# Seven block products in all three down products, roots by ScalarE, and the first up weights split ahead of the sums

## The chip, the cores and the metric

The kernel runs on one NeuronCore of a Trainium2 chip. TensorE (PE) multiplies matrices into PSUM, VectorE (DVE) and ScalarE (ACT) work on SBUF and PSUM, GpSimd (POOL) on SBUF, and SyncE (SP) issues nearly all DMAs. Each engine takes its instructions in a fixed order and waits on semaphores. The metric is the time of one execution on the device in microseconds (us), lower being better.

## The reference, cut to what matters

Two transformer blocks on 1024 tokens of width 1024, all in fp32. The first has three mixers (a state space model, a Fourier mixer, a banded attention) and a feed-forward part with a convolution over the tokens; the second has a feed-forward part, a two-branch attention, a second feed-forward part and a gate. The change touches the three feed-forward parts and the root in the norms:

```python
def rms_norm(x, gain):
    xf = x.astype(jnp.float32)
    y = xf * lax.rsqrt(jnp.mean(xf * xf, axis=-1, keepdims=True) + RMS_EPS)
    return (y * gain.astype(jnp.float32)).astype(x.dtype)
...
def dwconv3(h, w, b):
    hp = jnp.pad(h, ((0, 0), (1, 1), (0, 0)))
    return hp[:, :-2] * w[0] + hp[:, 1:-1] * w[1] + hp[:, 2:] * w[2] + b
...
        up = dwconv3(h @ w_up[l], conv_w[l], conv_b[l])          # first block, D_FF = 2816
        gate, val = jnp.split(up, 2, axis=-1)
        y = (jax.nn.gelu(gate) * val) @ w_down[l]
        x = x + gt_f * rms_norm(y, g_post_ffn[l])
...
def swiglu(x, w_gu, w_down):                                      # second block, twice
    g, u = jnp.split(x @ w_gu, 2, axis=-1)
    return (jax.nn.silu(g) * u) @ w_down
```

## The kernel before, in words

Every fp32 operand of a matmul is split into a high part (ACT copies it to fp32r) and a low part (DVE subtracts), and a product is three matmuls: high by high, low by high, high by low (`split`, L58 and L59; `mm3`, L96 to L98). The stages run one after another: the first mixer up to about 516 us, the feed-forward part with the convolution (ffn0 here) to about 1234, ffn1 to about 1885, the attention and its projection to about 2420, ffn2 and the gate to the end.

`ffn` is called for all three. It begins with four up tiles (hidden blocks 0 and 1) by plain products in four quarters of the tokens (`quarters`); their weights fill all four places of the tags `wh` and `wl`. Then it makes sums of the activation's quarters (L264 to L268, split into `S` and the `hl` of the old tiles), and for each further hidden block j a loop step: `weights(j)` loads two blocks of the up weight, makes four sums of them on POOL and splits all into `wh`, `wl` (three places each) and a tile `b`, and seven block products of 12 matmuls each (L297) stand for the eight of two by two blocks. `finish_tile` applies SiLU, or in ffn0 the convolution (L314 to L316) and GELU, and writes the block to DRAM.

For the down product ffn1 and ffn2 already use seven products (a Strassen scheme of Winograd's form): pairs of hidden blocks 2 to 19 in a group of four and one of five, seven chains of matmuls in each (`chain`, L445), fed by `blocks`, which loads the parts of a block one chain ahead (L431): parts of `hidden`, of the sums `hsum`, of `w_down` and of the sums `wsum`. The sums are made in the up loop. Of blocks 0, 1, 20 and 21 the product is plain and ends each part. ffn0 has no such sums and does all blocks in plain products of two blocks at a time (`down`), and the last four in one.

A part ends with its tail: for each of 8 token tiles the last sums into `yacc` (L406), the mean square on ACT (L145), a root on DVE (`rstd`, L121 to L128: a starting value from the integer bits and three Newton steps on 128x1 tiles), scaling (L1865), adding (L1866), a second mean square and root, the norm (L153) and transposes on PE (L180) split into `hh` and `hl` of the next part. `rstd` is called twice per tile.

The order of each engine's instructions is fixed when the kernel is built, by a scheduler that follows the code's order and data. Buffers are pools by tag: `raw` 3, `wh` and `wl` 4, `hh` and `hl` 2, `b4` (named `b` in the trace) 12. A tile that asks for a place waits for the last use of the tile before it.

Of the kernel before, what the change touches and what calls it, by code (L numbers as in the profile page):

```python
# [5 lines left out]
F32 = mybir.dt.float32  # L6
# [13 lines left out]
def f(ap):  # L20
    return ap.bitcast(F32)


class Core:
    def __init__(self, tc, ctx, ident, wbufs=4):
        self.tc, self.nc, self.ctx = tc, tc.nc, ctx
        nc = tc.nc
        self.g = ctx.enter_context(tc.tile_pool(name="g", bufs=1))
        self.ps = ctx.enter_context(tc.tile_pool(name="ps", bufs=1, space=PSUM))
        self.dr = ctx.enter_context(tc.tile_pool(name="dr", bufs=1, space=DRAM))  # L30

        for name, n, bufs in (("ss", 1, 4), ("rs_a", 1, 4), ("rs_i", 1, 4), ("rs_t", 1, 4), ("st0", 48, 2), ("st1", 48, 2)):
            self.g.tile([P, n], I32 if name == "rs_i" else F32, name=name, tag=name, bufs=bufs)
        self.A = [self.g.tile([P, 2, 24], F32, name=f"A{i}") for i in range(2)]
        self.taps = self.g.tile([P, 4, 44], F32, name="taps")
        self.cc = self.g.tile([P, 8], F32, name="cc")
        self.g.tile([P, 8], F32, name="gap")
        self.ones = self.g.tile([P, P], F32, name="ones")
        self.ident = self.g.tile([P, P], F32, name="ident")
        nc.sync.dma_start(self.ident, ident)  # L40
        self.wbufs = wbufs
        self.tmps, self.nrows = 4, 3
        self.pend = []
        self.tail = None
        self.rows = []
        self.tmptag = "tmp"
        self.counted = 0
# [69 lines left out]
    def rstd(self, ss):  # L117

        v = self.nc.vector
        s = self.g.tile([P, 1], F32, name="rs_a", tag="rs_a", bufs=4)  # L120
        v.tensor_scalar(s, ss, EPS, None, op0=OP.add)  # L121
        i = self.g.tile([P, 1], I32, name="rs_i", tag="rs_i", bufs=4)
        v.tensor_scalar(i, s.bitcast(I32), -0.5, float(0x5F3759DF), op0=OP.mult, op1=OP.add)
        y = i.bitcast(F32)
        t = self.g.tile([P, 1], F32, name="rs_t", tag="rs_t", bufs=4)
        for c in (3.0, 12.0, 768.0):
            v.tensor_scalar(t, y, y, s, op0=OP.mult, op1=OP.mult)  # L127
            v.tensor_scalar(y, t, c, y, op0=OP.subtract, op1=OP.mult)  # L128
        return y
# [54 lines left out]
def ffn(k, hT, w_gu, w_down, nff, prep, finish, taps=None, then=None):  # L184
# [5 lines left out]


    nc, v, pool = k.nc, k.nc.vector, k.nc.gpsimd
    pairs = list(range(2, nff - 2, 2)) if taps is None else []
    with k.tc.tile_pool(name="ffn", bufs=1) as fp:
        k.places(fp, "b4", 12)
        hidden = k.dr.tile([nff, P, D], F32, name=f"hidden{k.count()}")
        if pairs:
            hsum = k.dr.tile([2 * len(pairs), P, D], F32, name=f"hsum{k.count()}")
            wsum = k.dr.tile([2 * len(pairs), P, D], F32, name=f"wsum{k.count()}")

        def b4(dt=F32):
            return fp.tile([P, D], dt, name="b4", tag="b4", bufs=12)
# [54 lines left out]
        up, dn = slice(0, 4), slice(4, 8)  # L257
        A11, A12, A22, S4 = (h0[:, up], l0[:, up]), (h0[:, dn], l0[:, dn]), (h1[:, dn], l1[:, dn]), (h1[:, up], l1[:, up])
        S1, S2, S3 = [(t[:, 0], t[:, 1]) for t in sums]
        for a in range(0, 4, 2):  # L260
            c = slice(a, a + 2)
            x21, x22, x11, x12 = xs = [b4().rearrange("p (a b) -> p a b", a=2) for _ in range(4)]
            for x, (hi, lo) in zip(xs, (S4, A22, A11, A12)):
                v.tensor_tensor(x, f(hi[:, c]), f(lo[:, c]), op=OP.add)  # L264
            v.tensor_tensor(x22, x21, x22, op=OP.add)
            v.tensor_tensor(x21, x11, x21, op=OP.subtract)
            v.tensor_tensor(x11, x22, x11, op=OP.subtract)
            v.tensor_tensor(x12, x12, x11, op=OP.subtract)  # L268
            for x, (hi, lo) in ((x22, S1), (x11, S2), (x21, S3), (x12, S4)):
                k.split(hi[:, c], lo[:, c], x)  # L270

        def weights(j):

            rg, rv = k.raw([P, 8, P]), k.raw([P, 8, P])
# [16 lines left out]
            return dict(B11=both(W1, up), B21=both(W1, dn), T1=both(W2, up), T2=both(W2, dn), T3=both(W3, up),  # L291
                        B22=both(W3, dn), T4=(t4[:, 0], t4[:, 1]))

        def prod(ps, w, x, start):
            for a in range(4):
                for n, (y, z) in enumerate(((0, 0), (0, 1), (1, 0))):
                    nc.tensor.matmul(ps, w[y][:, a], x[z][:, a], start=start and a == 0 and n == 0, stop=a == 3 and n == 2,  # L297
                                     skip_group_check=True)
# [3 lines left out]
        def finish_tile(j, A, w, s, V):  # L302

            prod(A, w["T4"], A22, False)
            if taps is None:
                nc.scalar.activation(s[:, hi], A, AF.Silu)
                v.tensor_tensor(s[:, hi], s[:, hi], V[:, hi], op=OP.mult)
            else:
                nc.scalar.activation(s[:, hi], A, AF.Copy)
                us = []  # L310
                for m, z in ((j, s), (j + nff, V)):
                    u = b4()
                    t = [taps[:, a, m:m + 1] for a in range(4)]
                    nc.scalar.activation(u, z, AF.Identity, bias=t[3], scale=t[1])  # L314
                    v.scalar_tensor_tensor(u[:, 1:], z[:, :D - 1], t[0], u[:, 1:], op0=OP.mult, op1=OP.add)
                    v.scalar_tensor_tensor(u[:, :D - 1], z[:, 1:], t[2], u[:, :D - 1], op0=OP.mult, op1=OP.add)  # L316
                    us.append(u)
                s = us[0]
                nc.scalar.activation(s, s, AF.Gelu_apprx_tanh)
                v.tensor_tensor(s, s, us[1], op=OP.mult)  # L320
            nc.sync.dma_start(hidden[j], s)
            if pairs:
                made[j] = s

        made = {}

# [19 lines left out]

        prev = None
        for j in range(2, nff):
            w = weights(j)
            A, B, C = k.mm(), None, None  # L350
            X = b4()
            prod(A, w["B11"], A11, True)
# [11 lines left out]
            nc.scalar.activation(X[:, hi], C, AF.Copy)  # L364
            prod(A, w["T2"], S2, False)
            nc.scalar.activation(X[:, lo], A, AF.Copy)
            if j - 2 in pairs:
                weight_sums(j - 2)
            if j - 3 in pairs:
                hidden_sums(j - 3)  # L370
# [13 lines left out]
        def load(j):  # L384
# [6 lines left out]
            w = k.wide()  # L391
            k.split(*w, r)
            return h + w

        def down(ready, first, last):
            for i in range(NT):
                t = slice(i * P, i * P + P)
                for n in range(2):
                    c = slice(n * 512, n * 512 + 512)
                    po = k.mm()  # L400
                    for a, (hh, hl, wh, wl) in enumerate(ready):
                        k.mm3(po, (hh[:, t], hl[:, t]), (wh[:, c], wl[:, c]), a == 0, a == len(ready) - 1)
                    if first:
                        nc.scalar.activation(yacc[i][:, c], po, AF.Copy)
                    else:
                        v.tensor_tensor(yacc[i][:, c], yacc[i][:, c], po, op=OP.add)  # L406
                if last:
                    finish(fp, i, yacc[i])
                    if i >= 4:
                        k.flush(2, 1)  # L410

        def sources(name, j):

# [23 lines left out]
        def group(first):  # L437

            def chain(banks, h, c, start, new):
                ops = next(ahead)  # L440
                for i, po in enumerate(banks):
                    t = slice(i * P, i * P + P)
                    for m, (x, y) in enumerate(ops):
# [20 lines left out]
            chain(U, 1, hi, False, False)  # L464
            chain(U, 1, lo, False, True)

        groups = [pairs[:len(pairs) // 2], pairs[len(pairs) // 2:]] if pairs else []
        if pairs:
            def one_ahead(g):
                was = next(g)  # L470
                for x in g:
                    yield was
                    was = x
                yield was

            ahead = one_ahead(blocks())
            for a in range(2):
                group(a == 0)
        plain = [j for j in range(nff) if j - j % 2 not in pairs]
        n = len(plain) - 4  # L480
        for j in range(0, n, 2):
            down([load(j) for j in plain[j:j + 2]], j == 0, False)
        rows = big([4, D], F32)
        k.rows = [rows[:, a] for a in range(3)]
        k.junk = rows[:, 3]
        prep(fp)
        down([load(j) for j in plain[n:]], False, True)
        k.close()
        if then is not None:
            then(fp)  # L490
        k.rows = []
# [372 lines left out]
def project(k, mT, w, order, prep, finish, nrows):  # L864
# [4 lines left out]
    with k.tc.tile_pool(name="proj", bufs=1) as pp:  # L869
# [3 lines left out]
        for kt in order:  # L873
            r = k.raw([P, D])
            nc.sync.dma_start(r, w[kt * P:(kt + 1) * P, :])
            wh = pp.tile([P, D], F32R, name=f"woh{kt}")
            wl = pp.tile([P, D], F32R, name=f"wol{kt}")
            k.split(wh, wl, r)
            ws[kt] = (wh, wl)
        for i in range(NT):  # L880
            t = slice((i % 4) * P, (i % 4) * P + P)
            hi, lo = mT[i // 4]
# [13 lines left out]
            k.flush(1)  # L896
            finish(pp, i, y)
        k.close()

# [424 lines left out]
def mixers1(k, x, ada, p, prep, finish):  # L1326
# [345 lines left out]
    with tc.tile_pool(name="zo", bufs=1) as zo:  # L1672
# [13 lines left out]
                    next(gate, None)  # L1686

        prev = None
        for i in range(NT):
            y = k.tmp(zo)  # L1690
            for n, po in enumerate(product(i, (7, 0, 1, 2) if i < len(yp) else (3, 4, 5, 6, 7, 0, 1, 2))):
# [7 lines left out]
            prev = y  # L1699
        close(NT - 1, prev)  # L1700
        k.close()
    part.__exit__(None, None, None)
    outer.__exit__(None, None, None)
    return tabs
# [262 lines left out]
```

## Time and profile before

| | |
|---|---|
| median of 3 runs | 3171.17 us (3169.51 to 3174.13) |
| profiled execution, its own time | 3171.55 us |
| its span, first to last instruction | 3169.8 us |
| PE busy | 3027.8 us, 96% |
| DVE, ACT, POOL busy | 2156.8, 1327.4, 570.2 us |
| mean granted clock of PE | 0.978 of 2.4 GHz |

The span is one execution; all times in rows count from its start. Busy times are averages over stages of quite different kind, so the stages are read apart, in the rows further down.

### The profile page before, as it was taken

What the parts mean: (1) busy time and instruction counts of PE and PEld (TensorE: products, weight loads), DVE (VectorE), ACT (ScalarE), POOL (GpSimd) and SP (SyncE); (2) the same over time, 40 slices, a digit from 0 to 9 for tenths busy, and PEclk for the clock granted to TensorE, in tenths of its full rate; (3) what the DMA queues carried; (4) which work ended last, traced back from release to release, by engine and by line L of the source; (5) the groups of instructions that cost most, each with busy time, mean ns of one, the idle gap of its engine ahead of it and who ended that gap; (6) DMA issues with size and microseconds to landing.
All of it is one profiled execution on the core that took longest, in us unless ns stands there. A gap on an engine that the chain in (4) does not pass through costs nothing.

```text
span 3169.8 us, 40772 instructions
## 1 busy us (share of the span) xinstructions
PE 3027.8 (96%) x15146; PEld 2472.9 (78%) x15146; DVE 2156.8 (68%) x3750; ACT 1327.4 (42%) x2029; POOL 570.2 (18%) x823
## 2 busy tenths in 40 slices
PE   5889989799999998999999989999999999999998
PEld 3667668688887887888888878777779888888887
DVE  7866669866666669655556676666678655556687
ACT  4334643445444113433335434555742433335333
POOL 3468700222220000222220000000000222220000
PEclk8899999899999999999999999999999999999999
DMA  7474455122224232344458432210451344458434
GB/s 210 165 206 154 145 171 160 60 80 83 84 88 145 87 127 100 120 166 160 159 191 298 143 121 87 67 45 32 163 205 67 127 159 160 166 199 302 157 132 160
DMA packets 323578, 447.83 MB, mean 141 GB/s; under 512 B 40167, under 2 KB 213479, under 8 KB 323378
## 3 DMA queue, kind: packets, MB, share of 16 engines
q1 hardware_dynamic: 314914, 430.68, 40.7%
q10 hardware_dynamic: 6576, 9.00, 0.8%
q0 software_dynamic: 1888, 5.53, 0.7%
q8 instruction: 119, 1.95, 0.2%
q14 instruction: 81, 0.66, 0.1%
HBM read 322.02 MB, written 129.41 MB: 142 GB/s over the span
## 4 chain that ended last, share of the span: by engine, by line
PE 76%; DVE 9%; POOL 5%; DMA 2%; ACT 2%; issue 2%; ACTq 0%; DVEq 0%; SPq 0%; POOLq 0%
PE mm L297 36%; PE mm L445 9%; PE mm L96 7%; PE mm L98 7%; PE mm L97 7%; PE tp L445 2%; PE mm L644 2%; PE mm L606 2%; PE tp L632 2%; POOL X L1204 1%; POOL st L1201 1%; POOL X L1203 1%; POOL st L1202 1%; DVE rs_t L127 1%; DVE tmp L1866 1%
## 5 line engine op out<-in xcount | busy, mean ns | idle before, releaser
L297 PE MATMUL mm<-S,wh 128*128 128x512 f32 x1440 | 444.4, 390 | 8.1 <-ACT wh L58 4.9
L278 POOL TENSOR_TENSOR b<-raw 128x512 f32<-128x512 f32 x60 | 77.7, 1294 | 1485.4 <-PE tp L180 788.2
L58 ACT ACTIVATE wh<-raw 128x1024 fp32r<-128x1024 f32 x208 | 218.3, 1055 | 286.0 <-PE mm L297 133.7
L297 PEld LDWEIGHTS mm<-S,wh 128*128 128x128 f32 x1440 | 270.2, 188 | 65.7 <-ACT wh L58 5.3
L96 PE MATMUL mm<-hh,wh 128*128 128x256 f32 (+1 forms) x880 | 300.3, 341 | 18.8 <-ACT hh L58 15.0
L59 DVE TENSOR_TENSOR wl<-raw,wh 128x1024 fp32r<-128x1024 f32 x206 | 274.6, 1334 | 44.5 <-ACT wh L58 44.2
L97 PE MATMUL mm<-hl,wh 128*128 128x256 f32 (+1 forms) x880 | 298.2, 339 | 3.5 <-DVE hl L59 3.5
L98 PE MATMUL mm<-hh,wl 128*128 128x256 f32 (+1 forms) x880 | 297.3, 339 | 0.4 <-DVE wl L59 0.4
L297 PE MATMUL mm<-hh,wl 128*128 128x512 f32 x720 | 281.3, 391 | 9.3 <-DVE wl L59 9.3
L297 PE MATMUL mm<-hh,wh 128*128 128x512 f32 x720 | 281.1, 390 | 0.0
L297 PE MATMUL mm<-hl,wh 128*128 128x512 f32 x720 | 280.9, 390 | 0.0
L297 PE MATMUL mm<-S,wl 128*128 128x512 f32 x720 | 280.1, 389 | 0.0
L96 PEld LDWEIGHTS mm<-hh,wh 128*128 128x128 f32 x880 | 170.6, 194 | 36.3 <-ACT hh L58 15.3
L96 PE MATMUL mm<-wh,b 128*128 128x512 f32 x480 | 188.6, 394 | 4.0 <-ACT b L58 4.0
L287 POOL TENSOR_TENSOR b<-raw,b 128x512 f32<-128x512 f32 x60 | 81.6, 1360 | 606.6 <-DVE wl L59 606.6
L97 PE MATMUL mm<-wl,b 128*128 128x512 f32 x480 | 188.6, 393 | 0.0
L98 PE MATMUL mm<-wh,b 128*128 128x512 f32 x480 | 186.5, 390 | 0.0
L97 PEld LDWEIGHTS mm<-hl,wh 128*128 128x128 f32 x880 | 170.9, 194 | 18.5 <-DVE hl L59 4.1
L98 PEld LDWEIGHTS mm<-hh,wl 128*128 128x128 f32 x880 | 170.4, 194 | 17.6 <-DVE wl L59 1.2
L372 DVE TENSOR_TENSOR b<-mm,b 128x512 f32<-128x512 f32 x60 | 41.5, 691 | 199.4 <-PE mm L297 190.4
L297 PEld LDWEIGHTS mm<-hh,wl 128*128 128x128 f32 x720 | 135.9, 189 | 38.2 <-DVE wl L59 9.9
L297 PE MATMUL mm<-hh,b 128*128 128x512 f32 x480 | 157.9, 390 | 0.8 <-DVE b L376 0.8
(416 smaller groups left out, 7074.7 us busy)
## 6 DMA issues: line engine op xcount, KB each, us to landing
raw<-in_ffn_w_gu SPq DMA_DIRECT2D x88, 512.0 KB
hidden<-b SPq DMA_DIRECT2D x66, 512.0 KB
raw<-in_w_ada SPq DMA_DIRECT2D x48, 512.0 KB
raw<-in_w_up SPq DMA_DIRECT2D x44, 512.0 KB
x<-tmp SPq DMA_DIRECT2D x40, 512.0 KB
tmp<-x SPq DMA_DIRECT2D x40, 512.0 KB
b<-in_ffn_w_down SPq DMA_DIRECT2D x36, 512.0 KB
hsum<-b SPq DMA_DIRECT2D x36, 512.0 KB
```

Of the source, the lines that this page charges most:

```text
L58: self.nc.scalar.activation(hi, src, AF.Copy)
L59: (eng or self.nc.vector).tensor_tensor(lo, src, f(hi), op=OP.subtract)
L96: mm(out, a[0], b[0], start=start, stop=False)
L97: mm(out, a[0], b[1], start=False, stop=False)
L98: mm(out, a[1], b[0], start=False, stop=stop)
L278: pool.tensor_tensor(T[:, up], rv[:, up], rg[:, up], op=OP.subtract)
L287: pool.tensor_tensor(T[:, up], rg[:, dn], T[:, dn], op=OP.subtract)
L297: nc.tensor.matmul(ps, w[y][:, a], x[z][:, a], start=start and a == 0 and n == 0, stop=a == 3 and n == 2, skip_group_check=True)
L445: nc.tensor.matmul(po, x[a][:, t], y[b], start=start and m == 0 and z == 0, stop=m == len(ops) - 1 and z == 2, skip_group_check=True)
L606: nc.tensor.matmul(p[:, :nw], Q[a][:, s, q], K[s][:, k0 + c0:k0 + c0 + nw], start=a == 0, stop=a == 1)
L632: nc.tensor.transpose(tp[:, 2 * b + s], S[s][:, (b0 + b) * P:(b0 + b + 1) * P], k.ident)
L644: nc.tensor.matmul(po[s * 64:s * 64 + 64, q], V[:, tiles[j], vcol[s]:vcol[s] + 64], PT[:, 2 * b + s], start=j == 0, stop=j == nt - 1)
```

## The change

It has four parts. (1) ffn0 also uses the seven products for blocks 2 to 19; its weight sums for the second group (`late`) are made during the first five chains, and the four plain blocks come last in all parts. Hidden sums are made in ffn0's up loop as well. (2) Where `k.root` is set (the mixer's last loop, the tails of the three feed-forward parts, the projection), `rstd` takes ACT's square root, DVE's reciprocal and one Newton step in three operations. (3) In ffn0's convolution one of the two shifted taps goes through PSUM: ACT scales halves of it into `tp`, DVE adds them. (4) `weights(2)` stands ahead of the activation's sums in all three parts. Also, the last token tile's two halves are interleaved by block. From the diff:

```diff
@@ rstd
+        if self.root:
+            d = self.g.tile([P, 1], I32, name="rs_i", tag="rs_i", bufs=4).bitcast(F32)
+            self.nc.scalar.activation(d, ss, AF.Sqrt, bias=self.eps)
+            y = self.g.tile([P, 1], F32, name="rs_a", tag="rs_a", bufs=4)
+            v.reciprocal(y, d)
+            t = self.g.tile([P, 1], F32, name="rs_t", tag="rs_t", bufs=4)
+            v.tensor_scalar(t, ss, EPS, y, op0=OP.add, op1=OP.mult)
+            v.tensor_scalar(t, t, y, 3.0, op0=OP.mult, op1=OP.subtract)
+            v.tensor_scalar(y, t, y, 4096.0, op0=OP.mult, op1=OP.mult)
+            return y
@@ ffn
-    pairs = list(range(2, nff - 2, 2)) if taps is None else []
+    pairs = list(range(2, nff - 2, 2))
+    groups = [pairs[:len(pairs) // 2], pairs[len(pairs) // 2:]]
+    late = list(groups[1]) if taps is not None else []
...
-        for a in range(0, 4, 2):
...
+        first = weights(2)
+        for a in range(0, 4, 2):
...
-                    v.scalar_tensor_tensor(u[:, 1:], z[:, :D - 1], t[0], u[:, 1:], op0=OP.mult, op1=OP.add)
+                    for a, b in ((1, 512), (512, D)):
+                        q = k.ps.tile([P, 4, P], F32, name="tp", tag="tp", bufs=2).rearrange("p a b -> p (a b)")[:, :b - a]
+                        nc.scalar.activation(q, z[:, a - 1:b - 1], AF.Copy, scale=t[0])
+                        v.tensor_tensor(u[:, a:b], u[:, a:b], q, op=OP.add)
...
-            w = weights(j)
+            w = weights(j) if j > 2 else first
...
-            if j - 2 in pairs:
+            if j - 2 in pairs and j - 2 not in late:
                 weight_sums(j - 2)
...
             def chain(banks, h, c, start, new):
                 ops = next(ahead)
+                if late:
+                    weight_sums(late.pop(0))
...
-        n = len(plain) - 4
-        for j in range(0, n, 2):
-            down([load(j) for j in plain[j:j + 2]], j == 0, False)
...
-        down([load(j) for j in plain[n:]], False, True)
+        ready = [load(j) for j in plain]
+        k.root = True
+        for i in range(NT):
...
+            if i == NT - 1:
+                both.sort(key=lambda x: x[1])
```

The orders show what moves. First DVE at the start of ffn1, where the quarters' products with the up weights end (L245, after the change L258) and the activation's sums are made (adds L264 to L268, after it L300 to L304; L59 and L61 are the low splits). Before:

```order
L264 TENSOR_TENSOR b_10880<-hh,hl 128x1024
L265 TENSOR_TENSOR b_10878<-b_10877,b_10878 128x1024
L59 TENSOR_TENSOR wl<-raw,wh 128x1024
L266 TENSOR_TENSOR b_10877<-b_10879,b_10877 128x1024
L245 TENSOR_TENSOR b_10649<-b_10649,mm 128x512
L267 TENSOR_TENSOR b_10879<-b_10878,b_10879 128x1024
L59 TENSOR_TENSOR S<-b_10878,S 128x1024
L268 TENSOR_TENSOR b_10880<-b_10880,b_10879 128x1024
```

After:

```order
L258 TENSOR_TENSOR b_10725<-b_10725,mm 128x512
L258 TENSOR_TENSOR b_10728<-b_10728,mm 128x512
L61 TENSOR_TENSOR wl<-raw,wh 128x1024
L258 TENSOR_TENSOR b_10725<-b_10725,mm 128x512
L61 TENSOR_TENSOR wl<-b_10937,wh 128x1024
L300 TENSOR_TENSOR b_10957<-hh,hl 128x1024
L61 TENSOR_TENSOR b_10954<-b_10937,b_10954 128x512
L300 TENSOR_TENSOR b_10958<-hh,hl 128x1024
L61 TENSOR_TENSOR wl<-raw,wh 128x1024
L258 TENSOR_TENSOR b_10728<-b_10728,mm 128x512
```

Before, the low split of the first weights stands behind 15 of the 26 operations on the sums; after, it and that of the second (`wl<-b`) stand ahead of the first add.

Second SP at the end of ffn0's up loop, after the change (L430 loads parts of a block of the chains, L338 writes a hidden block, L355 and L356 load and L360 and L361 write a weight sum; the first `b_8654`, `b_8659`, `b_8664` are the last three pairs of the first chain):

```order
L430 DMA raw<-hsum_5154 128x512
L430 DMA raw<-in_w_down 128x512
L338 DMA hidden_5153<-b_8511 128x1024
L430 DMA raw<-hsum_5154 128x512
L430 DMA b_8654<-hidden_5153 128x512
L430 DMA b_8654<-in_w_down 128x512
L430 DMA b_8659<-hidden_5153 128x512
L430 DMA b_8659<-in_w_down 128x512
L430 DMA b_8664<-hidden_5153 128x512
L430 DMA b_8664<-in_w_down 128x512
```

and some twenty rows on:

```order
L360 DMA wsum_5155<-b_8691 128x1024
L430 DMA b_8774<-hsum_5154 128x512
L430 DMA b_8774<-wsum_5155 128x512
L361 DMA wsum_5155<-b_8692 128x1024
L355 DMA b_8779<-in_w_down 128x1024
L356 DMA b_8780<-in_w_down 128x1024
L430 DMA b_8852<-hsum_5154 128x512
L430 DMA b_8852<-in_w_down 128x512
```

Before, the same place held for each block a load of `hidden` and one of `w_down`:

```order
L321 DMA hidden_5200<-b_8288 128x1024
L386 DMA raw<-hidden_5200 128x1024
L390 DMA raw<-in_w_down 128x1024
L321 DMA hidden_5200<-b_8381 128x1024
L386 DMA raw<-hidden_5200 128x1024
L390 DMA raw<-in_w_down 128x1024
```

Loads of parts and of weight sums now share the queue, and writes that wait for DVE stand between them.

Third DVE in the tail from ffn0 to ffn1. Before:

```order
L153 SCALAR_TENSOR_TENSOR S<-tmp,rs_i,S 128x1024
L127 TENSOR_SCALAR rs_t<-rs_i,rs_a 128x1
L121 TENSOR_SCALAR rs_a<-ss 128x1
L59 TENSOR_TENSOR hl<-tp,hh 128x4x128
L128 TENSOR_SCALAR rs_i<-rs_t,rs_i 128x1
L123 TENSOR_SCALAR rs_i<-rs_a 128x1
L59 TENSOR_TENSOR wl<-raw,wh 128x1024
L127 TENSOR_SCALAR rs_t<-rs_i,rs_a 128x1 x2
L128 TENSOR_SCALAR rs_i<-rs_t,rs_i 128x1 x2
```

After (`rs_i` is now ACT's root, L124):

```order
L126 RECIPROCAL rs_a<-rs_i 128x1
L61 TENSOR_TENSOR hl<-tp,hh 128x4x128
L128 TENSOR_SCALAR rs_t<-ss,rs_a 128x1
L1885 TENSOR_TENSOR tmp<-tmp,S 128x1024
L129 TENSOR_SCALAR rs_t<-rs_t,rs_a 128x1
L61 TENSOR_TENSOR hl<-tp,hh 128x4x128
L130 TENSOR_SCALAR rs_a<-rs_t,rs_a 128x1
```

Eight small operations per root have become four, still mixed with the other work of the tail.

## Rows read from the trace of the kernel before

**Rows 1.** The page: busy us, share and instructions; chain that ended last.

```profile
PE 3027.8 (96%) x15146; PEld 2472.9 (78%) x15146; DVE 2156.8 (68%) x3750; ACT 1327.4 (42%) x2029; POOL 570.2 (18%) x823
PE 76%; DVE 9%; POOL 5%; DMA 2%; ACT 2%; issue 2%; ACTq 0%; DVEq 0%; SPq 0%; POOLq 0%
```

**Rows 2.** The chain in order of time: start us, us, what.

```profile
597.07 369.32 PE mm L297 x1628
...
1284.34 8.20 PE mm L297 x36
1293.16 370.21 PE mm L297 x1632
```

**Rows 3.** Stretches: us, busy us of each engine, PE clock, DMA share, GB/s.

```profile
1200.00:1250.00 50.00, 40.30 (x236) 34.92 (x235) 47.94 (x129) 22.58 (x38) 0.00 (x0) 0.86 0.40 137
1860.00:1910.00 50.00, 40.81 (x212) 34.25 (x211) 49.72 (x136) 22.04 (x36) 0.00 (x0) 0.83 0.39 136
470.00:530.00 60.00, 54.71 (x292) 45.56 (x291) 58.49 (x136) 23.55 (x41) 0.00 (x0) 0.97 0.55 173
```

**Rows 4.** Timeline of PE at ffn0's start: start, us, operation, [idle before, releaser].

```profile
574.08 1.22 PE L297 MATMUL mm<-S,wh 128*128 128x512 f32 x2 [4.91 <-ACT wh L58]
...
584.57 0.80 PE L297 MATMUL mm<-hh,wl 128*128 128x512 f32 x1 [9.27 <-DVE wl L59]
...
597.07 0.73 PE L297 MATMUL mm<-S,wh 128*128 128x512 f32 x2 [1.94 <-ACT b L353]
```

**Rows 5.** The chain at the end of ffn0's up loop.

```profile
967.16 3.05 PE mm L297 x12
...
974.23 0.79 PE mm L96
975.02 0.43 PE mm L97
```

**Rows 6.** Timeline of DVE at ffn1's start.

```profile
1256.24 3.49 DVE L264 TENSOR_TENSOR b<-hh,hl 128x1024 f32<-128x1024 f32 x3
...
1275.64 1.22 DVE L265 TENSOR_TENSOR b<-b,b 128x1024 f32<-128x1024 f32 x1
1276.77 1.22 DVE L59 TENSOR_TENSOR wl<-raw,wh 128x1024 fp32r<-128x1024 f32 x1
...
1280.78 1.22 DVE L59 TENSOR_TENSOR S<-b,S 128x1024 fp32r<-128x1024 f32 x1
```

**Rows 7.** Timeline of ACT there.

```profile
1275.62 1.06 ACT L58 ACTIVATE wh<-raw 128x1024 fp32r<-128x1024 f32 x1 [4.66 <-PE mm L97]
...
1278.56 1.06 ACT L58 ACTIVATE wh<-b 128x1024 fp32r<-128x1024 f32 x1 [0.45 <-PE mm L97]
```

**Rows 8.** A stretch of ffn0's up loop, columns as in rows 3.

```profile
597.00:897.00 300.00, 299.93 (x1323) 248.38 (x1324) 201.00 (x189) 146.39 (x175) 87.27 (x66) 1.00 0.27 86
```

**Rows 9.** Timeline of DVE in ffn0's tail.

```profile
1194.06 0.27 DVE L127 TENSOR_SCALAR rs_t<-rs_i,rs_a 128x1 f32<-128x1 f32 x1
1194.24 0.14 DVE L121 TENSOR_SCALAR rs_a<-ss 128x1 f32<-128x1 f32 x1
1194.36 0.21 DVE L128 TENSOR_SCALAR rs_i<-rs_t,rs_i 128x1 f32<-128x1 f32 x1
1194.49 0.14 DVE L123 TENSOR_SCALAR rs_i<-rs_a 128x1 int32<-128x1 int32 x1
```

**Rows 10.** Groups by line, DVE, 1185 to 1245: busy us, mean ns, idle.

```profile
L121 DVE TENSOR_SCALAR rs_a<-ss 128x1 f32<-128x1 f32 x15 | 2.2, 146 | 0.2
```

**Rows 11.** One line's instructions: ns min/median/max, first and last start.

```profile
L236 ACT ACT_TABLE_LOAD  x1: 1283/1283/1283, 564.3 to 564.3; - x1
```

**Rows 12.** Timeline of SP's DMA issues at the end of ffn1's up loop.

```profile
1656.19 0.43 SPq L431 DMA_DIRECT2D b<-in_ffn_w_down  x1
```

**Rows 13.** Timeline of ACT there.

```profile
1662.24 1.06 ACT L58 ACTIVATE hh<-b 128x1024 fp32r<-128x1024 f32 x1 [3.61 <-DMA b<-in_ffn_w_down]
```

**Rows 14.** Two stretches, columns as in rows 3.

```profile
1175.00:1180.00 5.00, 5.00 (x24) 4.05 (x23) 2.06 (x3) 0.93 (x1) 0.00 (x0) 1.00 1.03 372
2850.00:2900.00 50.00, 50.00 (x221) 41.05 (x220) 29.23 (x29) 27.39 (x34) 0.00 (x0) 1.00 0.90 316
```

More of the change, by code (lines that the diff above doesn't have):

```diff
@@ L36, in __init__ @@
         self.cc = self.g.tile([P, 8], F32, name="cc")
-        self.g.tile([P, 8], F32, name="gap")
+        self.eps = self.g.tile([P, 8], F32, name="eps")[:, :1]
+        nc.vector.memset(self.eps, EPS)
+        self.root = False
         self.ones = self.g.tile([P, P], F32, name="ones")
@@ L196, in ffn @@
         hidden = k.dr.tile([nff, P, D], F32, name=f"hidden{k.count()}")
-        if pairs:
-            hsum = k.dr.tile([2 * len(pairs), P, D], F32, name=f"hsum{k.count()}")
-            wsum = k.dr.tile([2 * len(pairs), P, D], F32, name=f"wsum{k.count()}")
+        hsum = k.dr.tile([2 * len(pairs), P, D], F32, name=f"hsum{k.count()}")
+        wsum = k.dr.tile([2 * len(pairs), P, D], F32, name=f"wsum{k.count()}")
         def b4(dt=F32):
@@ L259, in ffn @@
         S1, S2, S3 = [(t[:, 0], t[:, 1]) for t in sums]
-        for a in range(0, 4, 2):
[L261 to L270, printed above, removed]
         def weights(j):
@@ L292, in weights @@
                         B22=both(W3, dn), T4=(t4[:, 0], t4[:, 1]))
+        first = weights(2)
+        for a in range(0, 4, 2):
+            c = slice(a, a + 2)
+            x21, x22, x11, x12 = xs = [b4().rearrange("p (a b) -> p a b", a=2) for _ in range(4)]
+            for x, (hi, lo) in zip(xs, (S4, A22, A11, A12)):
+                v.tensor_tensor(x, f(hi[:, c]), f(lo[:, c]), op=OP.add)
+            v.tensor_tensor(x22, x21, x22, op=OP.add)
+            v.tensor_tensor(x21, x11, x21, op=OP.subtract)
+            v.tensor_tensor(x11, x22, x11, op=OP.subtract)
+            v.tensor_tensor(x12, x12, x11, op=OP.subtract)
+            for x, (hi, lo) in ((x22, S1), (x11, S2), (x21, S3), (x12, S4)):
+                k.split(hi[:, c], lo[:, c], x)
         def prod(ps, w, x, start):
@@ L321, in finish_tile @@
             nc.sync.dma_start(hidden[j], s)
-            if pairs:
-                made[j] = s
+            made[j] = s
         made = {}
@@ L393, in load @@
             return h + w
[L395 to L410, printed above, removed]
         def sources(name, j):
@@ L465, in group, with one_ahead @@
             chain(U, 1, lo, False, True)
[L467 to L473, printed above, removed]
-                yield was
-            ahead = one_ahead(blocks())
-            for a in range(2):
-                group(a == 0)
+        def one_ahead(g):
+            was = next(g)
+            for x in g:
+                yield was
+                was = x
+            yield was
+        ahead = one_ahead(blocks())
+        for a in range(2):
+            group(a == 0)
         plain = [j for j in range(nff) if j - j % 2 not in pairs]
-        n = len(plain) - 4
-        for j in range(0, n, 2):
-            down([load(j) for j in plain[j:j + 2]], j == 0, False)
         rows = big([4, D], F32)
@@ L486, in ffn @@
         prep(fp)
-        down([load(j) for j in plain[n:]], False, True)
+        ready = [load(j) for j in plain]
+        k.root = True
+        for i in range(NT):
+            t = slice(i * P, i * P + P)
+            both = [(n, a) for n in range(2) for a in range(4)]
+            if i == NT - 1:
+                both.sort(key=lambda x: x[1])
+            po = {}
+            for n, a in both:
+                hh, hl, wh, wl = ready[a]
+                c = (lo, hi)[n]
+                if not a:
+                    po[n] = k.mm()
+                k.mm3(po[n], (hh[:, t], hl[:, t]), (wh[:, c], wl[:, c]), a == 0, a == 3)
+                if a == 3:
+                    v.tensor_tensor(yacc[i][:, c], yacc[i][:, c], po[n], op=OP.add)
+            finish(fp, i, yacc[i])
+            if i >= 4:
+                k.flush(2, 1)
         k.close()
+        k.root = False
         if then is not None:
@@ L879, in project @@
             ws[kt] = (wh, wl)
+        k.root = True
         for i in range(NT):
@@ L898, in project @@
         k.close()
+        k.root = False
 def bucket(d):
@@ L1688, in mixers1 @@
         prev = None
+        k.root = True
         for i in range(NT):
@@ L1701, in mixers1 @@
         k.close()
+        k.root = False
     part.__exit__(None, None, None)
```

## The prediction

> **What bounds the kernel now.** I read the page first [rows 1]: TensorE (PE) is busy 96% of the span, and the chain that ended last lies 76% on PE, 9% on VectorE (DVE). A microsecond off PE's queue is therefore a microsecond off the time, wherever PE is not waiting. Then the chain in order of time [rows 2]: in the three long up loops nothing but L297 stands. 1628 matmuls in 369.32 us are 0.2268 us each, the price of a 128x512 matmul below. At the start of ffn1 PE runs 36 of them, pauses 0.62 us and goes on. Third, the stretches around the stage changes [rows 3]: from 1200 to 1250 (ffn0's tail into ffn1) PE has 40.30 of 50 us at a mean granted clock of 0.86 while DVE has 47.94; from 1860 to 1910 (ffn1 into the attention) 40.81 at 0.83 and DVE 49.72; from 470 to 530 (first mixer into ffn0) 54.71 of 60 and DVE 58.49. There DVE sets the pace. Last, two places where PE waits for other things: at the start of ffn0's up loop 4.91 + 9.27 + 1.94 = 16.1 us [rows 4], and from ffn0's up loop to its down product, where L297 ends at 970.21 and the next matmul starts at 974.23, at first at 0.43 us each, the 1.2 GHz level [rows 5]: 4.0 us idle and ten matmuls 0.2 too long, some 2.3, together 6.3.
>
> **Seven products in ffn0.** Blocks 2 to 19 cost 18 x 8 x 2 x 3 = 864 matmuls before and 7 x 48 + 7 x 60 = 756 after. 108 x 0.2268 = 24.5 us gained if the chains are fed.
>
> **Weights ahead of the sums, ffn1 and ffn2.** Before, DVE makes the activation's sums while PE still runs the quarters: the first add starts at 1256.24, the second half of S1 is split at 1280.78 [rows 6]. After, the order puts W1's low split, an L258 and W2's low split in front of the first add. W1 goes into a wh/wl place of the quarters' weights, and that is free only when PE has done with it: ScalarE's (ACT) split of it starts at 1275.62, having waited for PE, and W2's at 1278.56 [rows 7]. Behind that waiting split stand all sums and the last two L258, which free the quarters' PSUM banks; PE, whose next products read S, waits for them. So DVE stands still for some 18 us that it used, and starts at 1275.62 + 1.06 = 1276.7. Up to and with the second half of S1 the order then has 22 operations of 1024 columns at 1.135 us (1275.64 to 1276.77, [rows 6]) and 4 of 512 at about 0.60: 25.0 + 2.4, with 1.9 for the waits on W2's place and on GpSimd's T4, some 29.3, so 1306.0. The halves of S2, S3 and S4 follow, the last at about 1312.9 (six such operations). PE needs them from 1284.34 + 24 x 0.2268 = 1289.8 on. Before, its first 80 matmuls end at 1284.34 + 0.62 + 80 x 0.2268 = 1303.1; after, some 17 of the 80 stand behind the last half, so 1312.9 + 3.9 = 1316.8. Lost: 13.7 us, and the same in ffn2, whose orders read alike: 27.4. If the 17 run at 0.43 it is 3.4 more each; if PE's order hides some sums, 3 less. A gain is excluded, since PE waits only 0.62 us there now.
>
> **The same at ffn0.** Here PE waits already, and DVE has taps to work on meanwhile. By the same count the second half of S1 comes at about 596 and S4's at 603, the first 80 matmuls end near 607.5 against 604.8: 2.7 lost (6 lost to 2 gained, since the pieces of the quarters move too).
>
> **Conv and hidden sums.** The tap becomes two ACT copies and two DVE adds; the sums add 2.45 us of DVE to every second tile. In 300 us of this loop PE has 299.93, DVE 201.00, ACT 146.39 [rows 8]. By the durations of like rows ACT gets 4 x 0.6 us per tile of 18.9 us, some 38 us more, and DVE some 10 more: still far under 300, cost nothing. Were that cover gone, it would be up to 2.4 us per tile.
>
> **Roots.** A root is now L121, L123 and three pairs of L127, L128, and the next starts 0.18 after L127, 0.12 after L121, 0.13 after L128 [rows 9]; with 0.12 for L123 too that is 3 x 0.31 + 0.24 = 1.17 us of DVE. After, it is a reciprocal and three such operations, not in the trace, bounded by the nearest rows: 4 x 0.12 to 4 x 0.18, so 0.48 to 0.72; I take 0.63, four times the rows' mean (0.55) and 0.08 for what of the wait on ACT's root isn't covered. That saves 0.54. 15 roots stand in the tail from 1185 to 1245 [rows 10]: 8.1 us of a DVE that is never free, and PE idles over 9 there. So 8.1 each in ffn0's and ffn1's tails (3 to 10). In the mixer's tail PE lacks only 60 - 54.71 = 5.3; I take 3.5 (0 to 5.3). The projection and ffn2's tail have next to no idle PE: nothing. Tails together: 19.7.
>
> The root also switches ACT's table: by the two orders 19 loads for 8, at 1.283 us [rows 11]. ACT is 42% busy and a tail begins with its switch while the chain's matmuls still run: nothing (0 to 4 x 1.28 lost in ffn2's tail, where roots and sigmoids alternate). The Trainium skill's ScalarE: Activation LUTs, "What ACT_TABLE_LOAD costs", counts a drain too, 2.66 us for a switch, and asks to batch by set; by it those four would be 10.6 and the sum 3179. The trace of before shows the load alone.
>
> **Feeding ffn0's chains.** Two things are late. First, SP's order places a raw<-hsum (block 5's first load, whose place waits for block 2's first split, and that for the last up matmuls) ahead of block 1's loads into b4. They go out some 3.3 us after the up loop, take 1656.19 to 1662.24 = 6.05 in ffn1 [rows 12, 13], and need a split of 1.06; 12 matmuls (2.7) lie beside them: 7.5 lost. Second, six blocks of eight 262 KB loads (12.6 MB) and five weight sums of four 524 KB transfers (10.5 MB) share one queue in six chains of 48 x 0.2268 = 10.9 us. 23.1 MB in 65.3 us wants 354 GB/s. The trace reached 372 in one stretch of 5 us, but 316 over 50 us of ffn2's chains [rows 14]: 62 us or 73 us. I take the latter, as it is the same work: 7.8 late. With 2.3 for the slow clock after a gap as in rows 5: 17.6 against 6.3 before, 11.3 lost. Ends: 7 (all fed, the first loads late) and 28 (every wait of a sum's writes on DVE held up the queue). The Trainium skill's DMA: Bandwidth & Descriptors, "Bandwidth", gives about 358 GB/s as a core's share of HBM; by it the second part is nothing, and the sum 3160. The 372 GB/s agrees roughly, the 316 says that these loads don't reach it.
>
> **The sum.** 24.5 + 19.7 - 27.4 - 2.7 - 11.3 = 2.8 us faster. Against the profiled execution's 3171.55 that is 3168.7; this execution lies 0.4 above the median of the runs shown, so 3168.
>
> **Rivals.**
> *The chains are fed (24%).* For it: 372 GB/s was seen, and ffn1's chains start with no gap. Against: those had all sums made before. Only the first loads late gives 3168 - 10 = 3158, nothing late 3150.
> *ffn0's chains starve (16%), slower.* One mechanism: a wsum write in SP's queue waits for DVE's four subtractions on data just loaded, and the next block's loads stand behind it, five times over; 28 us instead of 17.6 make 3179, and beyond 25 lost it decides for slower. For it: SP's order interleaves them so. Against: ffn1's up loop does the same unharmed, with more time.
> *The roots give nothing (10%).* ACT's root is one more hop in a chain that DVE takes in order; a 0.5 us wait per root eats the 0.54. Then the tails' 19.7 go and it is 3188, with half of it 3178. For it: DVE waits for ACT's mean square in tails already. Against: other work stands between in the order.
> *The weights in front don't delay (4%).* If the places of the quarters' weights came free earlier than rows 7 show, 3141. Rows 7 speak against it.
>
> **How the numbers follow.** The sum as worked out gets 46%, its own range 3161 to 3177. A measurement of this kernel can tell about 0.2%, 6.3 us. Faster than that: 13 of the 46, 23 of the fed chains, the 4: 40%. Within: 31 of the 46, and one each of three rivals: 34%. Slower: 2, 15 and 9: 26%. The range 3150 to 3186 leaves out the last rival, the deep ends of fed chains and of useless roots, some 17%.
>
> **What would show it.** In the profile after: an idle PE of 10 us or more some 25 matmuls after the quarters of ffn1 and ffn2, released by DVE's split into S, with the clock at 0.5 beside it; DVE idle by 15 us before W1's split there; in ffn0 14 runs of 48 and 60 matmuls with gaps released by ACT's splits of loaded blocks, SP or DMA behind them; PE's busy time in 1860 to 1910's counterpart up by about 8. It is wrong if the sums still run beside the quarters, if ffn0's chains run without gaps, or if DVE's busy time per tail doesn't fall.

## The result, and the profile after

The changed kernel takes 3188.99 us (median of 4, 3186.36 to 3193.10) against 3172.17 for the kernel before on the same chip: ratio 1.0062, 95% interval 1.0049 to 1.0074, 17 us slower. The forecast was 3168 within 3150 to 3186. The time went into the starts of the up loops. From the trace, PE's first matmul of each up loop, the end of its 80th (the start of the next), and the loop's end:

| us | before | after | after less before |
|---|---|---|---|
| ffn0: first, 80th | 568.1, 606.3 | 566.0, 608.9 | -2.1, +2.7 |
| ffn0: loop's end | 970.0 | 973.7 | +3.7 |
| ffn1: first, 80th | 1284.2, 1303.3 | 1266.6, 1305.0 | -17.6, +1.7 |
| ffn1: loop's end | 1667.0 | 1668.7 | +1.7 |
| ffn2: first, 80th | 2466.0, 2485.1 | 2466.3, 2503.9 | +0.3, +18.8 |
| end of the span | 3169.8 | 3186.8 | +17.0 |

Up to ffn1's first up matmul the change is 17.6 us ahead. The next 80 matmuls take 38.4 us instead of 19.1 and give all of it back, and in ffn2 37.7 instead of 19.1. The page of the changed kernel, to [rows 1] (lines have moved: L297 is L311, L445 is L446, L59 is L61):

```profile
PE 3020.3 (95%) x15038; PEld 2457.4 (77%) x15038; DVE 2132.5 (67%) x3482; ACT 1433.8 (45%) x2227; POOL 600.0 (19%) x823
PE 68%; DVE 11%; POOL 6%; DMA 4%; issue 3%; ACT 3%; SPq 0%; DVEq 0%; ACTq 0%; POOLq 0%
```

PE has 108 matmuls less, but its part of the chain fell by 8 points: DVE and DMA gained 2 each, POOL, ACT and "issue" 1 each. PE's timeline at ffn1's start, where [rows 2] had one pause of 0.62 us (columns as in [rows 4]):

```profile
1274.42 0.47 PE L311 MATMUL mm<-S,wh 128*128 128x512 f32 x1 [2.21 <-issue]
...
1281.74 1.22 PE L311 MATMUL mm<-S,wh 128*128 128x512 f32 x2 [2.54 <-ACT b L369]
1288.01 0.80 PE L311 MATMUL mm<-S,wh 128*128 128x512 f32 x1 [3.34 <-ACT S L60]
1291.34 0.79 PE L311 MATMUL mm<-S,wh 128*128 128x512 f32 x1 [2.54 <-DVE S L61]
1294.65 0.80 PE L311 MATMUL mm<-S,wh 128*128 128x512 f32 x1 [0.80 <-ACT S L60]
```

PE idles 12.3 us in six waits, the last three for splits into S; what else is lost there is matmuls at a lower clock. Two stretches (columns as in [rows 3]): the granted clock is at its 1.2 GHz level, also in the first one after the waits.

```profile
1285.00:1290.00 5.00, 0.80 (x1) 0.29 (x1) 5.00 (x5) 2.46 (x3) 4.92 (x2) 0.50 0.00 0
1295.00:1300.00 5.00, 5.00 (x13) 3.86 (x13) 4.18 (x4) 1.14 (x2) 0.00 (x0) 0.53 0.00 0
```

ACT's split of the first weights, to [rows 7], and DVE's timeline, to [rows 6]:

```profile
1258.02 1.06 ACT L60 ACTIVATE wh<-raw 128x1024 fp32r<-128x1024 f32 x1 [16.56 <-PE mm L99]
```

```profile
1259.11 1.23 DVE L61 TENSOR_TENSOR wl<-raw,wh 128x1024 fp32r<-128x1024 f32 x1 [14.61 <-ACT wh L60]
...
1263.20 1.22 DVE L300 TENSOR_TENSOR b<-hh,hl 128x1024 f32<-128x1024 f32 x1
1266.27 0.69 DVE L61 TENSOR_TENSOR b<-b,b 128x512 fp32r<-128x512 f32 x1 [1.85 <-ACT b L60]
...
1289.00 2.28 DVE L61 TENSOR_TENSOR S<-b,S 128x1024 fp32r<-128x1024 f32 x1
1291.21 2.29 DVE L303 TENSOR_TENSOR b<-b,b 128x1024 f32<-128x1024 f32 x1
...
1297.97 1.21 DVE L61 TENSOR_TENSOR hl<-b,hh 128x1024 fp32r<-128x1024 f32 x1
```

DVE stands still for 14.61 us in front of the first low split, and the first add starts at 1263.20, where the quarters are nearly done. Before, it began 28 us ahead of the up loop's first matmul. Two operations take 2.28 and 2.29 instead of 1.22 us. POOL works beside them:

```profile
1277.91 10.08 POOL L279 TENSOR_TENSOR b<-raw 128x512 f32<-128x512 f32 x1 [12.34 <-DVE b L303]
1288.07 2.13 POOL L282 TENSOR_TENSOR b<-raw,b 128x512 f32<-128x512 f32 x1
1290.17 2.25 POOL L283 TENSOR_TENSOR raw<-raw 128x512 f32<-128x512 f32 x1
```

Before, POOL's sums for block 3 began 11.8 us after the up loop's first matmul, much as here (11.3), but DVE's last operation on the activation's sums had ended at 1288.54. POOL's took 1.29 to 1.30:

```profile
1295.96 1.29 POOL L278 TENSOR_TENSOR b<-raw 128x512 f32<-128x512 f32 x1 [4.01 <-DMA raw<-in_ffn_w_gu]
```

ffn1's tail, to the second of [rows 3], gained, with less busy DVE and a higher clock:

```profile
1860.00:1910.00 50.00, 42.59 (x245) 37.31 (x244) 46.92 (x97) 27.61 (x54) 0.00 (x0) 0.90 0.43 147
```

PE's busy time there is up by 1.8, where the prediction wanted about 8. From ffn1's loop to the attention's first matmul the change takes 266.3 us instead of 270.9.

### The profile page after: what moved, and what is told of

Same layout as the page of the kernel before. It is cut to its first block, busy times and chain, and to the rows that moved or that the text cites. A ratio compares the mean times of both kernels' runs of the same rounds, so it can differ in the third digit from the quotient of the medians.

```text
span 3186.8 us, 40562 instructions
## 1 busy us (share of the span) xinstructions
PE 3020.3 (95%) x15038; PEld 2457.4 (77%) x15038; DVE 2132.5 (67%) x3482; ACT 1433.8 (45%) x2227; POOL 600.0 (19%) x823
## 4 chain that ended last, share of the span: by engine, by line
PE 68%; DVE 11%; POOL 6%; DMA 4%; issue 3%; ACT 3%; SPq 0%; DVEq 0%; ACTq 0%; POOLq 0%
PE mm L311 35%; PE mm L446 11%; PE mm L100 4%; PE mm L98 4%; PE mm L99 4%; PE tp L446 3%; PE mm L659 2%; PE mm L621 2%; PE tp L647 2%; POOL X L1221 1%; POOL st L1218 1%; POOL X L1220 1%; POOL st L1219 1%; DVE tmp L1885 1%; DVE hl L61 1%
## 5 line engine op out<-in xcount | busy, mean ns | idle before, releaser
L311 PE MATMUL mm<-S,wh 128*128 128x512 f32 x1440 | 456.5, 397 | 42.4 <-ACT S L60 15.0
L279 POOL TENSOR_TENSOR b<-raw 128x512 f32<-128x512 f32 x60 | 104.3, 1738 | 1466.6 <-PE tp L192 921.3
L311 PEld LDWEIGHTS mm<-S,wh 128*128 128x128 f32 x1440 | 274.7, 191 | 109.9 <-ACT S L60 19.7
L60 ACT ACTIVATE wh<-raw 128x1024 fp32r<-128x1024 f32 x190 | 200.2, 1056 | 323.3 <-PE mm L311 142.9
L61 DVE TENSOR_TENSOR wl<-raw,wh 128x1024 fp32r<-128x1024 f32 x188 | 257.3, 1368 | 80.4 <-ACT wh L60 80.0
L311 PE MATMUL mm<-S,wl 128*128 128x512 f32 x720 | 284.2, 395 | 0.0
L311 PE MATMUL mm<-hh,wh 128*128 128x512 f32 x720 | 282.9, 393 | 0.0
L311 PE MATMUL mm<-hl,wh 128*128 128x512 f32 x720 | 282.1, 392 | 0.0
L311 PE MATMUL mm<-hh,wl 128*128 128x512 f32 x720 | 281.0, 391 | 0.0
L446 PE MATMUL mm<-hh 128*128 128x512 f32 x528 | 203.8, 392 | 5.2 <-ACT hh L60 5.2
L446 PE MATMUL mm<-hl,hh 128*128 128x512 f32 x528 | 205.4, 391 | 2.5 <-DVE hl L61 2.4
L446 PE MATMUL mm<-hh,hl 128*128 128x512 f32 x528 | 204.6, 389 | 0.0
L100 PEld LDWEIGHTS mm<-hh,wl 128*128 128x128 f32 x880 | 170.1, 194 | 22.7 <-DVE wl L61 6.5
L61 DVE TENSOR_TENSOR hl<-b,hh 128x1024 fp32r<-128x1024 f32 x132 | 155.8, 1221 | 29.1 <-ACT hh L60 28.9
L311 PEld LDWEIGHTS mm<-S,wl 128*128 128x128 f32 x720 | 137.7, 191 | 28.6
```

The source lines that it names most:

```text
L60: self.nc.scalar.activation(hi, src, AF.Copy)
L61: (eng or self.nc.vector).tensor_tensor(lo, src, f(hi), op=OP.subtract)
L100: mm(out, a[1], b[0], start=False, stop=stop)
L279: pool.tensor_tensor(T[:, up], rv[:, up], rg[:, up], op=OP.subtract)
L446: nc.tensor.matmul(po, x[a][:, t], y[b], start=start and m == 0 and z == 0, stop=m == len(ops) - 1 and z == 2, skip_group_check=True)
```

## The experiments

Each run stands beside the kernel before on its own chip; medians of that one were 3169 to 3172.

**e1, the sums first again.** The changed kernel without `first = weights(2)`, and `w = weights(j)` for all j.

> The changed kernel with its first up weights back behind the activation's sums; all else stays. Theory A (the starts carry the loss as the changed kernel's trace shows it: 80 matmuls of the up loop later by 19.3 us in ffn1, 18.6 in ffn2, 4.7 in ffn0): 3189 - 43 = 3146, and PE idle under 1 us at the starts of ffn1 and ffn2. Rival B (the starts lose the 13.7, 13.7 and 2.7 of the prediction, and the rest of the loss lies in the tails and the chains): 3159.

Measured 3142.68, ratio 0.9910 (0.9894 to 0.9926). In ffn1 PE's only wait at the start is again ACT's L353 of before, 0.6 us (columns: who waited for whom, total us, times, longest):

```profile
PE mm L310 <- ACT b L368: 0.6, 1, 0.6
```

Theory A holds: without this one part the change is 0.9% faster than before.

**e2, the weights ahead alone.** The kernel before with only that part.

> The kernel before with nothing changed but the first up weights put ahead of the sums. Theory A: 3172 + 19 + 19 + 3 to 5 = 3213 to 3215, with DVE idle some 14 us ahead of the first low split in ffn1. Rival B: 3172 + 13.7 + 13.7 + 2.7 = 3202. If the loss came only together with the other parts, 3172.

Measured 3216.32, ratio 1.0143 (1.0124 to 1.0161): 47 us lost, by the trace 5.4 at ffn0's start, 19.4 at ffn1's and 19.3 at ffn2's. The prediction's sizes (B) are too small.

**e6, halfway.** `if a == 2: first = weights(2)` within the sums' loop.

> The changed kernel with the first up weights between the two halves of the activation's sums instead of ahead of both. Theory A (the loss is the DVE work on the sums that is pushed behind the wait for the quarters' places): 12 of 26 operations, some 14 us, now run before the wait, so each of the starts of ffn1 and ffn2 loses about 5 instead of 19: 3189 - 28 = 3161, with ffn0 a little better. Rival (the wait itself on the weights' places costs, whatever stands behind it): 3189.

Measured 3152.53, ratio 0.9945 (0.9930 to 0.9959): 36 better than the change. The activation's sums are 24 operations in the traces, 12 in each half (before, 16 of the 24 stood ahead of the first weights' low split, not 15 of 26). The first 80 matmuls take 25.0 us in ffn1 and 24.8 in ffn2, a loss of 5.9 and 5.7, and 31.0 in ffn0, where before they took 38.2, in the change 42.9 and in e1 33.5. So the loss follows the amount of DVE work behind the wait, not the wait as such. The time lies 8 under theory A's 3161 because ffn0's start gains 11.9 too; that the weights are better ahead of half the sums there than behind all, 31.0 for 33.5, shows again in the trace of e10, 32.0 for the 33.5 of e5.

**e9, no POOL beside the delayed sums.** The four sums of `weights(3)` as ACT copies.

> The changed kernel, with the four sums of up weights on POOL left out for block 3 in each part (ACT copies one operand instead, so hidden block 3 is another). Theory (POOL's sums for block 3, which in the changed kernel fall into the delayed activation sums, slow DVE: two operations there take 2.28 and 2.29 us against 1.21): each start of ffn1 and ffn2 better by 2 to 3 us, ffn0 by 1: 3189 - 6 = 3183, with DVE's operations back at 1.2 us. Rival (they were slow for another reason): 3189.

Measured 3178.59, ratio 1.0024 (1.0014 to 1.0035). DVE's operations at the same place:

```profile
1286.09 1.22 DVE L61 TENSOR_TENSOR S<-b,S 128x1024 fp32r<-128x1024 f32 x1
1287.22 1.22 DVE L307 TENSOR_TENSOR b<-b,b 128x1024 f32<-128x1024 f32 x1
```

The starts got shorter by 3.1, 2.8 and 2.9 us. POOL's part of the loss is shown; it is the smaller one.

**e3, the roots alone.**

> The kernel before with nothing changed but the roots. Theory A (the tails gain some 2 + 4 + 4.5, half of what was forecast, since the order of DVE puts low splits of weights behind the norms): 3172 - 10 = 3162. The prediction's sum: 3172 - 19.7 = 3152. Rival B (roots on ACT give nothing, their waits eat the gain): 3172 or more.

Measured 3151.42, ratio 0.9940 (0.9926 to 0.9955), 17.7 faster. Theory A falls: from the changed kernel's tails I had read too little; the prediction's 19.7 is nearer in sum.

**e8, the old root in the projection.** e1 without `k.root = True` there.

> The kernel of e1 with the old root in the projection's tail alone. In e1 PE waits there 3.2 us for a low split of transposes that stands behind roots on DVE, and runs 5 us at a clock of 0.67; before it waited under 0.2. Theory (where DVE isn't the bound, the hop to ACT and back makes its queue wait): e1 - 4, 3139. Rival (the wait comes from elsewhere): 3143.

Measured 3137.06, ratio 0.9896 (0.9881 to 0.9911), 5.6 less than e1. In e1 the projection's tail has this wait, which e8 has not:

```profile
2386.16 1.68 PE L192 MATMUL tp<-ident,tmp 128*128 128x128 f32 x8 [3.20 <-DVE hl L61]
```

The intervals of the two runs overlap, but the traces place a gain there: from the end of ffn1's chains to ffn2's up loop e8 takes 625.9 us and e1 629.3. From the attention's last matmul to ffn2's up loop it is 144.4 before, 148.7 in e3, 149.1 in e1 and 145.5 in e8. The mechanism of the theory isn't what they show. DVE in e1, then in e8:

```profile
2383.00 1.23 DVE L1884 TENSOR_TENSOR tmp<-tmp 128x1024 f32<-128x1024 f32 x1 [3.90 <-DMA tmp<-x]
2384.14 1.28 DVE L910 TENSOR_TENSOR tmp<-mm,brow 128x512 f32<-128x512 f32 x2
2385.34 1.27 DVE L61 TENSOR_TENSOR hl<-tp,hh 128x512 fp32r<-128x512 f32 x2
2386.97 0.16 DVE L126 RECIPROCAL rs_a<-rs_i 128x1 f32<-128x1 f32 x1 [0.35 <-ACT rs_i L124]
```

```profile
2382.58 1.28 DVE L61 TENSOR_TENSOR hl<-tp,hh 128x512 fp32r<-128x512 f32 x2
2383.94 0.15 DVE L133 TENSOR_SCALAR rs_a<-ss 128x1 f32<-128x1 f32 x1
2384.05 1.23 DVE L1883 TENSOR_TENSOR tmp<-tmp 128x1024 f32<-128x1024 f32 x1
```

With the new root the order puts the adding of `x` (L1884) ahead of the splits that PE waits for, and it waits 3.90 us for the load of `x`; with the old root the splits stand ahead of it. For ACT's root DVE waits 0.35 us. Over e1's projection DVE's waits for these loads are 20.1 us in all and those for ACT's root 3.9; in e8 those for the loads are 2.0. That the order alone makes the loss wasn't run by itself.

**e4, seven products alone.** e1 with `k.root` never true.

> The kernel before with the seven products in ffn0, the tap through PSUM and the interleaved last tile, but old roots and the first weights behind the sums. Theory A (24.5 of matmuls saved, the chains' gaps 7 us longer than the old one): 3172 - 17 = 3155. The prediction's sum: 24.5 - 11.3, 3159. Chains that cost as much as they save: 3172.

Measured 3155.03, ratio 0.9948 (0.9930 to 0.9966): 14.1 faster, between theory A's 17 and the prediction's 13.2.

**e5, no sums beside the chains.** e1 with `late = []`.

> The kernel of e1 with all weight sums of ffn0 made in its up loop, none beside the chains. If the sums' transfers and their waits in SP's queue make the later gaps of ffn0's chains (in e1 4.0 us of the 7.8 idle, from 1003 on, and slow matmuls behind them), those go: e1 - 5, 3138. If the chains only lack their first loads: as e1, 3143. If the up loop, with ten more transfers and twenty more subtractions, holds PE up: 3148 or more.

Measured 3132.62, ratio 0.9879 (0.9862 to 0.9895), 10 better than e1, of which the traces place 5.8 between ffn0's up loop and ffn1's (290.6 in e1, 284.9 here). PE's waits in ffn0's chains, first e1's, then e5's:

```profile
PE mm L445 <- ACT hh L60: 3.5, 4, 1.4
PE mm L445 <- DVE hl L61: 2.4, 3, 1.2
PE tp L445 <- DVE b L331: 1.9, 1, 1.9
```

```profile
PE tp L445 <- DVE b L331: 1.9, 1, 1.9
PE mm L445 <- ACT hh L60: 0.9, 1, 0.9
PE mm L445 <- DVE hl L61: 0.5, 1, 0.5
```

The late gaps are gone and the up loop pays nothing (398.8 us for e1's 399.1). What is left at the first chain is 3.3 us.

**e10, the best parts.** e5 with the old root in the projection, and in ffn0 alone `if a == 2 and taps is not None: first = weights(2)`.

> What the runs so far point to, in one kernel: seven products in all parts with all weight sums in the up loops, ACT's roots except in the projection, the first up weights behind the sums in ffn1 and ffn2 and between the sums' halves in ffn0. Theory (the parts add up): the kernel with no sums beside the chains, 3133, less 5.6 for the projection's root and 2.5 for ffn0's start (its first to 80th matmul took 31.0 us with the weights between the halves, 33.5 behind them): 3125. Rival (gains overlap): 3130 or more.

Measured 3126.15, ratio 0.9859 (0.9844 to 0.9874): 44 us faster than before. The sum of the parts, 3125, is met; the rival's 3130 is the end of the interval, so a small overlap isn't excluded.

**e12, e10 with old roots.**

> The kernel of e10 with the old roots everywhere. Theory (roots are worth about what they gave alone, 17.7, and the projection's part of it was a loss of 5.6 already taken away): e10 + 18. Rival (in this surrounding they are worth the half that the changed kernel's tails showed, some 10): e10 + 10.

Measured 3145.06, ratio 0.9920 (0.9906 to 0.9935): roots are worth 18.9 here.

**e11 and e13, low splits on POOL.** `k.load_up(..., pool)` for the first four up weights, in e11 in all parts, in e13 in ffn1 and ffn2.

> The kernel of e10 with the low splits of the four first up weights of each feed-forward part on POOL instead of DVE. Theory (the tails give less than DVE saves because these splits stand behind the roots and norms in DVE's order, and PE waits 2.84 us for one at the start of ffn1's quarters, then runs at the 1.2 GHz level): that wait goes, e10 - 4 for ffn1, up to 4 more for ffn0 and ffn2. Rival (POOL's operations slow DVE's at the same time, as in the starts): as e10 or slower.

> The kernel of e10 with the low splits of the first four up weights on POOL in ffn1 and ffn2 alone. In the run before, with them on POOL in all three parts, PE's wait for a low split at ffn1's start (2.84 us) was gone and ffn1's up loop began 6.6 us earlier against ffn0's end, but ffn0's start lost as much, where PE waited 6.70 us for a low split of the transposes. Theory (POOL slows DVE in ffn0's start, where DVE's taps run; in ffn1 the split's place in DVE's queue was the wait): e10 - 6, 3120. Rival (the gain in ffn1 was only the time that ffn0 had lost, given back): 3126.

Measured 3125.14 (0.9860, 0.9844 to 0.9877) and 3126.26 (0.9857, 0.9835 to 0.9879): no gain. In e13's trace the way from ffn0's up loop to ffn1's is 6.7 us shorter than in e10 (278.5 for 285.2, and 278.5 in e11), but ffn0's loop already ends 5.2 later there, although up to that point the two have the same orders. One execution's stages thus differ by that much from run to run, and the times can't tell a gain from none. DVE pays for POOL's splits again:

```profile
1190.90 3.31 DVE L1886 TENSOR_TENSOR tmp<-tmp,S 128x1024 f32<-128x1024 f32 x1
```

## Why the prediction was wrong, point by point

**The step that failed** is "Weights ahead of the sums": the mechanism stood, the size didn't. Forecast were 27.4 us in ffn1 and ffn2 and 2.7 in ffn0, 30.1; alone it measured 47 (e2), and taken out of the change 46 (e1, 3188.99 to 3142.68; on different chips, by the ratios 1.5%). The 17 between forecast and measurement are most of the miss of 20. By the traces of the change and of e1, 19.3 were lost in ffn1, 18.6 in ffn2 and 9.4 in ffn0. The rest of the change, forecast at 24.5 + 19.7 - 11.3 = 32.9, measured 26.4 (e1), and 32.9 is within that run's interval. At ffn1 19.3 were lost instead of 13.7. Counted from ACT's split of W1 (1258.02), the last half of S4 was ready after 41.2 us (1297.97 + 1.21), forecast 37.3 (1275.62 to 1312.9). Of these 3.9, 2.6 are DVE's operations beside POOL (2.28, 2.29 and one of 1.71 for 1.22), which the sum had at nothing, and about 1 is waits (2.9 for the 1.9 forecast, 1.85 of it for T4). In e9, without POOL's sums there, each start is 2.8 to 3.1 shorter. The rest, 1.9, is PE's restart: the clock was 0.53 until 1300, which the prediction had only in its bound (3.4 more each), not in its value. That POOL would come beside DVE could be read: in the order POOL's block 3 waits only for its data and a place, and the delay of DVE alone moved the sums into its time. The price stood in the trace of before: two splits in 3.45 us beside POOL, where two alone take 2.35.

```profile
1289.59 3.45 DVE L59 TENSOR_TENSOR wl<-raw,wh 128x1024 fp32r<-128x1024 f32 x2
1289.82 2.13 POOL L287 TENSOR_TENSOR b<-raw,b 128x512 f32<-128x512 f32 x1 [33.73 <-DVE wl L59]
```

The Trainium skill's SBUF — State Buffer, "Who interferes with whom", says that DVE and GpSimd share a pair of ports as an exclusive lock, and that a DVE tensor_tensor with both inputs in SBUF contends with GpSimd's reads. The trace agrees: 2.28 beside POOL's 2.13, 1.22 alone in e9, and POOL's L279 took 10.08 us while eight such operations of DVE ran back to back beside it, each at its 1.22 to 1.23. The prediction did not weigh this.

**Seven products, and feeding the chains:** forecast 24.5 less 11.3, 13.2; alone 14.1 (e4). Right in sum. The late part was the weight sums' traffic and waits, as said; e5 takes both away together, so it doesn't tell one from the other. The rate of 316 GB/s, from which the 7.8 came, was no bound: these chains ran 20 us at 404 in the change (columns as in [rows 3]):

```profile
1074.00:1094.00 20.00, 20.00 (x90) 16.57 (x89) 13.08 (x15) 9.77 (x11) 0.00 (x0) 1.00 1.05 404
```

The first loads were forecast at 7.5 (the terms as given add up to 7.7) and 2.3 for the slow clock. In e5 it is 3.3 us of idle in the first chain, 1.9 of it a wait for the last tap, which still held a `tp` bank of PSUM; with the slow clock the chains lose 7.1 (177.7 us for 752 matmuls at 0.2268).

**Roots:** forecast 19.7, alone 17.7 (e3), beside other parts 18.9 without the projection (e12 against e10), and 12.4 with it (e1 against e4). Right in sum for the roots alone, and that by luck, since its places were wrong both ways. By the traces of e3 and before, one execution each, 7.1 were gained from the first mean square of the mixer's last loop to ffn0's 80th up matmul (forecast 3.5), 6.8 from ffn0's up loop to ffn1's and 6.7 from ffn1's to the attention (8.1 each), and 2.0 from ffn2's up loop on (nothing). The projection was booked at nothing, "next to no idle PE", and lost 4.3 there; in e1 against e8 it is 3.6 by the traces and 5.6 by the times. DVE isn't the bound there (in e1 2.0 of the 5 us from 2380 on busy): it stood waiting for loads of `x`, in an order that had put the waiting addition first. The third rival, a wait for ACT's root that eats the gain, isn't what happened: in the change DVE waits for it 0.4 us in all in ffn0's tail and 0.4 in ffn1's.

**Conv and hidden sums:** ffn0's loop is 1.0 us longer from its 80th matmul on; the cover held, nearly.

**The table loads:** eight of the 19 stand in ffn2's tail and the gate, for roots and sigmoids in turn, and the changed kernel ends 1.8 us better from ffn2's up loop on. In its gate a load starts 0.02 us after the operation before it, and the next operation 0.01 us after the load's end:

```profile
3113.55 0.18 ACT L157 ACTIVATION_READ_ACCUMULATOR S<-S 128x1 f32 x1
3113.75 1.28 ACT L1828 ACT_TABLE_LOAD   x1
3115.04 0.60 ACT L1828 ACTIVATE tmp<-mm 128x512 f32<-128x512 f32 x1
```

The 2.66 us that the Trainium skill's ScalarE: Activation LUTs, "What ACT_TABLE_LOAD costs", gives for a switch don't appear.

**ffn0's start:** 4.7 lost against before, where 2.7 were forecast, within its bounds of 6. But the other parts make this start shorter, 33.5 us in e1 for before's 38.2, and against e1 the weights ahead cost 9.4, outside them: the term was sized by a start that the same change shortens.

The rivals of the same sign as the result, starved chains and useless roots, are not what made it slower: products alone gain 14.1 (e4), roots alone 17.7 (e3).

## What to carry to other kernels

An instruction that waits for a place in a full pool stops everything behind it on its engine: before moving a step forward in the code, read what will free its destination, and count the work behind it, not the step. When work is delayed, look at what runs on the other engines at the new time: a price read from a row holds only beside the same neighbours. An operation moved to another engine pays where the first engine is the bound; where it isn't, it can still change the order, so read what now stands, waiting, in front of the work that others need. And a sum that comes out right is checked term by term: terms that are wrong both ways can hide in it.

## What the runs showed of the hardware that was not expected

DVE's two-input operations of 1024 columns took 2.28 us beside POOL's of 512, and 3.31 beside POOL's splits of 1024, against 1.22 alone; POOL's took 2.13 for 1.29, and one took 10.08 while DVE ran on without a pause. Whether parts take something from each other isn't settled: roots alone gained 17.7 and products alone 14.1, both together (e1) 26.4, and the 5 between lie within the intervals of the three runs.
